# Who multiplies q and k by their reciprocal roots, and in which order: GpSimd and VectorE in a two-layer decoder trunk

## The chip, the cores and the metric

The kernel runs on one core of one Trainium2 chip. The metric is the device time of one execution in microseconds (us), median of three runs. A difference of 0.2% is about what a measurement of this kernel can tell from no change.

## The reference, cut to what matters

Two transformer layers over 512 tokens of width 1024. In both, the heads (64 wide) of q and k are normalised by their root mean square before attention:

```python
def rms_norm(x, gain):
    y = xf * lax.rsqrt(jnp.mean(xf * xf, axis=-1, keepdims=True) + EPS)
    return (y * gain)

# layer 0: 8 heads "A" (dilated windows), 8 heads "B" (window 128, 2 kv heads, sinks)
aq = rms_norm(aq.reshape(bsz, seq, N_HEADS_A, HEAD_DIM), a_q_gain)   # ak, bq, bk likewise
# layer 1: 16 heads "C" (forgetting attention)
q = rms_norm(proj[..., :w].reshape(bsz, seq, N_HEADS_C, HEAD_DIM), c_q_gain)   # k likewise
```

After each layer's attention there is an output projection and a squared-ReLU MLP (1024 to 4096 to 1024).

## The kernel before, in words

All large products are made in float32 from two parts, a rounded part (`whi`) and the rest (`wlo`), as three matmuls (L234 to L236, L165 to L169). The weights come by DMA into `wraw` (four buffers) and are split into `whi` and `wlo` (seven buffers each) by ScalarE, GpSimd or VectorE (L151, L153, L156). In the attention stages the pattern `PAT_ATT` gives every `whi` to GpSimd and the `wlo` by turns to VectorE and GpSimd.

`project` (L212) multiplies all four blocks of 128 tokens by a group of weight columns; the results stand in four PSUM banks `pj`. For a group of q and k its `use` calls `norm_heads` (L243):

- ScalarE copies the four banks to two tiles `qk` of shape [128 tokens, 2 blocks, 512 columns] and squares them (L250, L254); VectorE sums the squares by head (L255).
- `rsqrt_small` (L120) computes the reciprocal root on VectorE, eleven short instructions on up to 36 columns a token; its result is `rs` (in the first call `room`).
- `normalise` (L271) multiplies `qk` by `rs`, block by block, in place. `NORM = 'vgvg'` gives blocks 0 and 2 to VectorE and blocks 1 and 3 to GpSimd; each instruction takes all columns of its block (512, or 128 for the two k heads of B).

`norm_heads` is called eight times. In this text the calls are named **start** (A, first four heads: 256 columns of q and 256 of k; its multiplications are put off until the first v projection has ended, L283 and L524), **kB** (two k heads of B), **qB** (eight q heads of B), **A1** (A, last four heads) and **C0** to **C3** (layer 1, four heads each, q and k).

`prep_q` and `prep_k` (L293, L304) then transpose 128 columns, that is one pair of heads, of all four blocks on TensorE (`head_T`, L290: four transposes into one bank `qkT`), split the result on ScalarE and VectorE (L300, L301, L160, L161), and for k swap halves with a DMA (L313). The first pair needs columns 0 to 127 of q and, where q and k stand in one tile, columns 256 to 383 for k. Scores follow (L348 to L351), softmax (L362 to L373), transposes of the probabilities (L385), values (L405 to L409).

A generator `run` (L453) mixes steps of attention with matmuls of the next projection in program order. The order on each engine is then planned when the kernel is built, by program order and by the planner's own costs; only instructions under `in_order` or `keep_in_program_order` are pinned behind the one traced before them on their engine. [...]

Of the kernel before, what the change touches and what calls it, by code (L numbers as in the profile page):

```python
# [18 lines left out]
P = 128  # L19
# [3 lines left out]
NT = S // P  # L23
FF = 4096
HD = 64
# [9 lines left out]
R = 6  # L35
PAT_START = (('act', 'dve'), ('act', 'dve'))
WARM = 30
NORM = 'vgvg'
PSC = 'ggga'
GRAIN = 4  # L40
TABLES0 = 6
# [19 lines left out]
LEADS = (0.0, 0.0, -0.16, 0.33, -0.3, -0.23, -0.09)  # L61
# [8 lines left out]
def trunk(ctx, tc, x, b_sinks, w_out_even, b_forget, w_out_odd, w_up, w_down, xt, gains, w_in_even, w_in_odd, out):  # L70
    nc = tc.nc
# [72 lines left out]
    def in_order(m):  # L144
        if cnt["start"]:
            tc.keep_in_program_order(m)
# [50 lines left out]
    def layer_attention(li, hT, w_in, w_out, stats=None):  # L197


        with ExitStack() as c2:  # L200
# [39 lines left out]
                use(outs)  # L240
                yield 0

            def norm_heads(outs, nh, sq_tag="sq", sq_bufs=1 + li, ms=None):  # L243


                w = nh * HD
# [22 lines left out]
                                            op0=OP.mult, op1=OP.add)  # L269
                rsqrt_small(rs, v, room)  # L270
                def normalise():  # L271
                    for t in range(NT):
                        q = qk[t // 2][:, t % 2, :w].rearrange("p (h d) -> p h d", d=HD)
                        eng = nc.gpsimd if NORM[t] == "g" else nc.vector
                        m = eng.tensor_mul(q, q, rs[:, t, :nh].unsqueeze(2).to_broadcast([P, nh, HD]))
                        if eng is nc.vector:
                            in_order(m)

                if ms is None:
                    normalise()  # L280
# [168 lines left out]
            def chain(*gens):  # L449
                for g in gens:  # L450
                    yield from g

            def run(att, n_att, dense, n_dense, lead=0.0):  # L453

                a = d = 0
                while True:
                    if d / n_dense <= (a + lead * n_att) / n_att or att is None:
                        c = next(dense, None)
                        if c is None:
                            break  # L460
                        d += c
                    else:
                        if next(att, "end") == "end":
                            att = None
                        a += 1
                if att is not None:
                    for _ in att:
                        pass
# [56 lines left out]
                    cnt["start"] = False  # L525
                return use

            def qk_use(key, nh, *sq):
                def use(outs, ms=None):
                    st["qk", key] = norm_heads(outs, nh, *sq, ms=ms)  # L530
                return use

            def all_of(gen):
# [3 lines left out]
            if li == 0:  # L537
# [25 lines left out]

                start(ap, hT, w_in, make_tables(ap, dist, lt, lb), [bank("pA", f"pj{t}") for t in range(NT)], qk_use(0, 8, "P3", 2))
                all_of(v_a(0))
                run(att_a(0), 32, chain(kv_b(), project([(1536, 2048)], qk_use("b", 8))), 768, LEADS[0])
                run(att_b(), NB, chain(qk_a(1), v_a(1)), 768, LEADS[1])
                run(chain(att_a(1), last_values()), 38, chain(out_part([0, 1, 4, 5], True),
                                                              out_part([6, 7], False), ahead([2, 3])), 1536, LEADS[2])
# [714 lines left out]
```

## Time and profile before

| | us |
|---|---|
| median of the runs (three, 1161.77 to 1162.87) | 1161.94 |
| the profiled execution, its own time | 1160.99 |
| its span, first to last instruction | 1159.2 |

The span is nearly all TensorE: the two attention stages lie at about 28 to 215 us and 590 to 820 us, the MLPs behind them. The profiled execution is 0.95 us below the median.

### The profile page before, as it was taken

The numbers are of one execution on the slowest core, as the hardware profiler recorded it, in microseconds if no ns is written. First come the engines' busy times: TensorE is split into PE (matmuls) and PEld (weight loads), VectorE is DVE, ScalarE is ACT, GpSimd is POOL, SyncE is SP. The second block draws the span as 40 slices with busy tenths as digits, with TensorE's granted clock in tenths as the row PEclk, the third lists the DMA queues.
The fourth block names the chain that finished last, engine by engine and source line by source line (L and its number), as shares of the span: only waits on it lengthen the run. The fifth ranks groups of instructions, "written<-read, shape, count | busy, mean of one in ns | idle before, by whom it ended". The sixth has DMA issues, their size and how long they took to land.

```text
span 1159.2 us, 17365 instructions
## 1 busy us (share of the span) xinstructions
PE 1141.9 (99%) x6228; PEld 977.8 (84%) x6228; DVE 873.0 (75%) x1865; ACT 645.2 (56%) x1342; POOL 198.1 (17%) x292
## 2 busy tenths in 40 slices
PE   9999999999999999999999999999999999999998
PEld 7887887888989988988988888888888888888887
DVE  7878899969868857855647877778858759669676
ACT  7555867655545455444335685655756455465452
POOL 0445434100000000000255545332100000000000
PEclk9999999999999999999999999999999999999999
DMA  8432114232333332433443433343420722523403
GB/s 288 131 91 74 55 38 146 75 108 91 93 108 92 112 105 76 123 96 111 147 128 109 110 101 98 111 129 117 161 86 18 230 80 67 188 73 111 147 34 109
DMA packets 94695, 126.57 MB, mean 109 GB/s; under 512 B 5888, under 2 KB 66304, under 8 KB 94608
## 3 DMA queue, kind: packets, MB, share of 16 engines
q1 hardware_dynamic: 93568, 123.29, 34.7%
q10 hardware_dynamic: 1040, 2.16, 0.5%
q8 instruction: 49, 0.80, 0.3%
q14 instruction: 38, 0.31, 0.1%
HBM read 114.39 MB, written 4.23 MB: 102 GB/s over the span
## 4 chain that ended last, share of the span: by engine, by line
PE 84%; DVE 8%; DMA 3%; ACT 2%; issue 2%; POOL 1%; SPq 0%; POOLq 0%; DVEq 0%; ACTq 0%
PE up L165 10%; PE up L169 10%; PE up L168 10%; PE pj L236 4%; PE pj L234 4%; PE pj L235 4%; PE O L405 3%; PE PT L385 2%; PE op L169 2%; PE op L165 2%; PE op L168 2%; PE Y L1045 2%; PE Y L1042 2%; PE Y L1044 2%; PE Y L1091 1%
## 5 line engine op out<-in xcount | busy, mean ns | idle before, releaser
L165 PE MATMUL up<-xin,whi 128*128 128x512 f32 x512 | 200.6, 392 | 0.0
L169 PE MATMUL up<-xin,whi 128*128 128x512 f32 x512 | 199.4, 389 | 0.0
L168 PE MATMUL up<-xin,wlo 128*128 128x512 f32 x512 | 199.3, 389 | 0.0
L791 ACT CAST whi<-wraw 128x512 fp32r<-128x512 f32 x228 | 139.2, 619 | 105.1 <-PE up L169 47.7
L792 DVE TENSOR_TENSOR wlo<-wraw,whi 128x512 fp32r<-128x512 f32 x228 | 151.6, 685 | 50.9 <-ACT whi L791 50.7
L169 PEld LDWEIGHTS up<-xin,whi 128*128 128x128 f32 x512 | 96.1, 188 | 20.1
L168 PEld LDWEIGHTS up<-xin,wlo 128*128 128x128 f32 x512 | 96.2, 188 | 19.9 <-issue 0.2
L165 PEld LDWEIGHTS up<-xin,whi 128*128 128x128 f32 x512 | 96.2, 188 | 19.6 <-issue 0.2
L365 ACT ACTIVATE P<-P,negm 128x128 f32<-128x128 f32 (+5 forms) x128 | 69.5, 543 | 42.7 <-DVE negm L362 40.3
L973 ACT ACTIVATE u<-up 128x512 f32<-128x512 f32 x64 | 38.3, 598 | 90.9 <-PE up L169 90.9
L234 PE MATMUL pj<-whi,hn 128*128 128x512 f32 (+2 forms) x256 | 88.7, 347 | 0.0
L236 PE MATMUL pj<-whi,hn 128*128 128x512 f32 (+2 forms) x256 | 87.0, 340 | 0.0
L235 PE MATMUL pj<-wlo,hn 128*128 128x512 f32 (+2 forms) x256 | 86.9, 339 | 0.0
L153 POOL TENSOR_SCALAR whi<-wraw 128x512 fp32r<-128x512 f32 x88 | 59.7, 680 | 158.7 <-PE pj L236 137.6
L812 DVE TENSOR_TENSOR t<-u 128x256 f32<-128x256 f32 x56 | 23.2, 423 | 62.8 <-ACT u L1116 61.1
L156 POOL TENSOR_TENSOR wlo<-wraw,whi 128x512 fp32r<-128x512 f32 x48 | 63.8, 1332 | 21.4 <-ACT whi L151 18.9
L156 DVE TENSOR_TENSOR wlo<-wraw,whi 128x512 fp32r<-128x512 f32 (+1 forms) x71 | 49.0, 698 | 18.6 <-POOL whi L153 15.1
L373 POOL TENSOR_SCALAR P<-P,rden 128x256 f32<-128x256 f32 (+2 forms) x96 | 48.0, 503 | 82.8 <-DVE rden L368 77.2
L397 ACT CAST PT<-PT 128x256 fp32r<-128x256 f32 (+3 forms) x128 | 48.9, 403 | 20.3 <-PE PT L385 19.4
L362 DVE CUSTOM_DVE_ANT_0 P<-S,bias 128x128 f32<-128x128 f32 (+1 forms) x96 | 45.7, 484 | 17.4 <-PE S L351 11.8
L791 ACT CAST whi<-mraw 128x512 fp32r<-128x512 f32 x64 | 38.8, 620 | 33.1 <-DVE mraw L902 14.4
L385 PE MATMUL PT<-ident,P 128*128 128x128 f32 x296 | 53.4, 276 | 2.4 <-DVE negm L362 1.4
(241 smaller groups left out, 3083.5 us busy)
## 6 DMA issues: line engine op xcount, KB each, us to landing
wraw<-in_w_up SPq DMA_DIRECT2D x64, 512.0 KB, 4.3
wraw<-in_w_down SPq DMA_DIRECT2D x56, 512.0 KB, 3.8
wraw<-in_w_in_odd SPq DMA_DIRECT2D x22, 512.0 KB, 3.8
wraw<-in_w_in_even SPq DMA_DIRECT2D x17, 512.0 KB, 5.0
mraw<-in_w_down SPq DMA_DIRECT2D x16, 512.0 KB, 4.7
K<-K SPq DMA_DIRECT2D x26, 256.0 KB, 2.9
bias<-csp SPq DMA_DIRECT2D x16, 256.0 KB, 3.3
wraw<-in_w_out_odd SPq DMA_DIRECT2D x8, 512.0 KB, 3.7
```

The source lines that it names most:

```text
L153: nc.gpsimd.tensor_scalar(dst_h, src, 1.0, 1.0, op0=OP.mult, op1=OP.mult)
L156: in_order((nc.gpsimd if lo == "pool" else nc.vector).tensor_sub(dst_l, src, dst_h.bitcast(F32)))
L165: m = nc.tensor.matmul(o, wh, xh, start=start, stop=False, skip_group_check=more)
L168: nc.tensor.matmul(o, wl, xh, start=False, stop=False, skip_group_check=more)
L169: nc.tensor.matmul(o, wh, xl, start=False, stop=stop, skip_group_check=more)
L234: nc.tensor.matmul(o, xh, hi[:, :n], start=k == 0, stop=False)
L235: nc.tensor.matmul(o, xh, lo[:, :n], start=False, stop=False)
L236: nc.tensor.matmul(o, xl, hi[:, :n], start=False, stop=k == DC - 1)
L365: nc.scalar.activation(p[:, :ne], p[:, :ne], AF.Exp, scale=-1.0, bias=negm[:, i:i + 1], accum_out=den[:, i:i + 1])
L385: nc.tensor.transpose(pt[:, (i - c) * P:(i - c + 1) * P], pr[i][:, kb * P:(kb + 1) * P], ident)
L791: sca(nc.scalar.copy(dst_h, src))
L792: late.append(lambda: vec(nc.vector.tensor_sub(dst_l, src, dst_h.bitcast(F32))))
```

## The change

It takes the pattern by blocks away and deals the columns out instead. VectorE multiplies the columns of the first pair of heads in all four blocks (four instructions): of 512 columns the first 128 of each half for `halves=2` (256 columns in all), the first 128 for qB, which passes `halves=1`, and all 128 for kB. Then, for all but kB, VectorE copies the roots from `rs` into `v` (a tile of the same small size that is no longer needed), pinned behind its last multiplication, and GpSimd multiplies the other columns of the four blocks (256 each, or 384 for qB), reading the roots from that copy.

```diff
-NORM = 'vgvg'
-            def norm_heads(outs, nh, sq_tag="sq", sq_bufs=1 + li, ms=None):
+            def norm_heads(outs, nh, sq_tag="sq", sq_bufs=1 + li, ms=None, halves=1):
...
                 def normalise():
-                    for t in range(NT):
-                        q = qk[t // 2][:, t % 2, :w].rearrange("p (h d) -> p h d", d=HD)
-                        eng = nc.gpsimd if NORM[t] == "g" else nc.vector
-                        m = eng.tensor_mul(q, q, rs[:, t, :nh].unsqueeze(2).to_broadcast([P, nh, HD]))
-                        if eng is nc.vector:
-                            in_order(m)
+
+                    def mul(eng, hs, rs):
+                        for t in range(NT):
+                            q = qk[t // 2][:, t % 2, :w].rearrange("p (s h d) -> p s h d", s=halves, d=HD)[:, :, hs]
+                            r = rs[:, t, :nh].rearrange("p (s h) -> p s h", s=halves)[:, :, hs]
+                            m = eng.tensor_mul(q, q, r.unsqueeze(3).to_broadcast([P, halves, hs.stop - hs.start, HD]))
+                            if eng is nc.vector:
+                                in_order(m)
+
+                    mul(nc.vector, slice(0, 2), rs)
+                    if nh > 2 * halves:
+                        tc.keep_in_program_order(nc.vector.tensor_copy(v[:, :, :nh], rs[:, :, :nh]))
+                        mul(nc.gpsimd, slice(2, nh // halves), v)
...
-            def qk_use(key, nh, *sq):
+            def qk_use(key, nh, *sq, halves=2):
                 def use(outs, ms=None):
-                    st["qk", key] = norm_heads(outs, nh, *sq, ms=ms)
+                    st["qk", key] = norm_heads(outs, nh, *sq, ms=ms, halves=halves)
...
-                run(att_a(0), 32, chain(kv_b(), project([(1536, 2048)], qk_use("b", 8))), 768, LEADS[0])
+                run(att_a(0), 32, chain(kv_b(), project([(1536, 2048)], qk_use("b", 8, halves=1))), 768, LEADS[0])
```

## Rows read from the trace of the kernel before

**Rows 1.** The page, parts 1 and 2: TensorE's busy time with its share of the span and its count, and the clock granted to it in 40 slices (tenths of full speed).

```profile
PE 1141.9 (99%) x6228; PEld 977.8 (84%) x6228; DVE 873.0 (75%) x1865; ACT 645.2 (56%) x1342; POOL 198.1 (17%) x292
...
PEclk9999999999999999999999999999999999999999
```

**Rows 2.** The page, part 4: the chain of work that ended last, share of the span by engine.

```profile
PE 84%; DVE 8%; DMA 3%; ACT 2%; issue 2%; POOL 1%; SPq 0%; POOLq 0%; DVEq 0%; ACTq 0%
```

**Rows 3.** Who made TensorE wait over the whole span: us in total, times, longest.

```profile
PE S L348 <- DMA K<-K: 1.7, 2, 1.2
...
PE S L348 <- DVE yf L409: 1.2, 1, 1.2
PE qkT L290 <- DVE qk L275: 1.2, 2, 0.7
PE qkT L290 <- POOL qk L275: 1.1, 2, 0.5
```

**Rows 4.** The multiplications, all instructions of L275: duration in ns (least, median, most), first and last start, shapes. The two of `room` are those of start.

```profile
L275 DVE TENSOR_TENSOR qk<-qk,rs x14: 293/1138/1537, 67.5 to 752.9; 128x512 f32<-128x512 f32 x12, 128x128 f32<-128x128 f32 x2
L275 POOL TENSOR_TENSOR qk<-qk,rs x14: 435/1488/1549, 67.6 to 753.8; 128x512 f32<-128x512 f32 x12, 128x128 f32<-128x128 f32 x2
...
L275 POOL TENSOR_TENSOR qk<-qk,room x2: 1047/1048/1049, 39.2 to 40.2; 128x512 f32<-128x512 f32 x2
...
```

**Rows 5.** Timeline of qB, by engine (VectorE, GpSimd, TensorE): start, busy us, instruction, and in brackets the idle time before it with what ended it.

```profile
99.97 2.14 DVE L275 TENSOR_TENSOR qk<-qk,rs 128x512 f32<-128x512 f32 x2
...
100.02 2.99 POOL L275 TENSOR_TENSOR qk<-qk,rs 128x512 f32<-128x512 f32 x2 [0.52 <-DVE rs L135]
...
99.77 0.39 PE L236 MATMUL pj<-whi,h 128*128 128x512 f32 x1
100.81 0.30 PE L290 MATMUL qkT<-ident,qk 128*128 128x128 f32 x1 [0.65 <-DVE qk L275]
101.62 0.33 PE L290 MATMUL qkT<-ident,qk 128*128 128x128 f32 x1 [0.51 <-POOL qk L275]
...
102.25 0.27 PE L290 MATMUL qkT<-ident,qk 128*128 128x128 f32 x1
103.07 0.33 PE L290 MATMUL qkT<-ident,qk 128*128 128x128 f32 x1 [0.55 <-POOL qk L275]
```

**Rows 6.** Timeline of A1, VectorE and then TensorE, columns as in rows 5.

```profile
153.26 2.81 DVE L275 TENSOR_TENSOR qk<-qk,rs 128x512 f32<-128x512 f32 x2
156.10 0.68 DVE L409 TENSOR_TENSOR yf<-O,yf 64x512 f32<-64x512 f32 x1
...
155.21 0.40 PE L168 MATMUL op<-y,wlo 128*128 128x512 f32 x1
156.84 0.39 PE L348 MATMUL S<-K,Q 128*128 128x256 f32 x1 [1.23 <-DVE yf L409]
```

**Rows 7.** Timeline of start, GpSimd, VectorE and then TensorE, columns as in rows 5.

```profile
39.24 2.06 POOL L275 TENSOR_TENSOR qk<-qk,room 128x512 f32<-128x512 f32 x2 [1.57 <-issue]
41.27 1.20 POOL L153 TENSOR_SCALAR whi<-wraw 128x512 fp32r<-128x512 f32 x2
42.55 1.59 POOL L156 TENSOR_TENSOR wlo<-wraw,whi 128x512 fp32r<-128x512 f32 x1
...
41.92 1.09 DVE L156 TENSOR_TENSOR wlo<-wraw,whi 128x512 fp32r<-128x512 f32 x1 [0.73 <-POOL whi L153]
...
43.32 1.97 DVE L275 TENSOR_TENSOR qk<-qk,room 128x512 f32<-128x512 f32 x2
...
42.23 0.28 PE L234 MATMUL pj<-whi,h 128*128 128x256 f32 x1
43.45 0.39 PE L234 MATMUL pj<-whi,h 128*128 128x256 f32 x1 [0.95 <-DVE v L161]
...
44.03 0.28 PE L236 MATMUL pj<-whi,h 128*128 128x256 f32 x1
44.83 0.63 PE L290 MATMUL qkT<-ident,qk 128*128 128x128 f32 x4 [0.52 <-DVE qk L275]
```

**Rows 8.** Timeline behind the multiplications of C0 (GpSimd, VectorE, TensorE), and in the last line the same wait of VectorE behind C3.

```profile
611.91 0.62 POOL L153 TENSOR_SCALAR whi<-wraw 128x512 fp32r<-128x512 f32 x1
...
614.51 1.08 DVE L156 TENSOR_TENSOR wlo<-wraw,whi 128x512 fp32r<-128x512 f32 x1 [3.47 <-POOL whi L153]
...
619.08 0.39 PE L235 MATMUL pj<-wlo,hn 128*128 128x512 f32 x1
620.66 0.36 PE L348 MATMUL S<-K,Q 128*128 128x256 f32 x1 [1.20 <-DMA K<-K]
...
755.95 0.69 DVE L156 TENSOR_TENSOR wlo<-wraw,whi 128x512 fp32r<-128x512 f32 x1 [1.53 <-POOL whi L153]
```

**Rows 9.** Prices of like instructions. First the page's part 5 (busy us, mean ns of one): a product of 256 columns on VectorE; then two lines of instructions by source line or tile (ns least, median, most): the small copy behind the roots of start, and VectorE's `wlo` in the stage 28 to 215 us.

```profile
L812 DVE TENSOR_TENSOR t<-u 128x256 f32<-128x256 f32 x56 | 23.2, 423 | 62.8 <-ACT u L1116 61.1
...
L282 DVE COPY rcol<-room x1: 170/170/170, 39.1 to 39.1; 128x4 f32<-128x4 f32 x1
...
L156 DVE TENSOR_TENSOR wlo<-wraw,whi x24: 674/686/1524, 27.5 to 206.9; 128x512 fp32r<-128x512 f32 x24
```

**Rows 10.** Two loads into one tile `wraw`, whose column ranges (256 and 16 of each row of 272) interleave in it: issue of both on the DMA queue, and the time from issue to landing.

```profile
549.62 0.88 SPq L184 DMA_DIRECT2D wraw<-in_w_in_odd  x2
...
DMA to landing us min/median/max: 2.5/2.7/2.8
```

## The prediction

> **What bounds the kernel now.** I read the page first. [...] Second, the list of what TensorE waited for [rows 3]: the multiplications appear by name (1.2 us for VectorE's, 1.1 us for GpSimd's), and next to them waits that may hang on them (`yf`, the DMA of K). Third, the timelines around the eight calls, to see what each of these waits is. The ends of matmuls are modelled, so I take the lost time from start to start: matmuls of 512 columns follow each other at 0.23 us, of 256 at 0.12, transposes at 0.11.
>
> The reader is to see this in them. At **qB** four transposes stand in TensorE's queue ahead of projection work that could run, and block 0 waits for VectorE, blocks 1 and 3 for GpSimd. From 99.77 to 100.81, 100.81 to 101.62 and 102.25 to 103.07 that is 0.81 + 0.70 + 0.71 = 2.2 us lost [rows 5]. At **A1** the transposes come later; the loss is 155.21 to 156.84, 1.4 us, and it stands behind VectorE's `yf`, which waits in VectorE's queue behind 2.81 us of multiplications [rows 6]. At **start** TensorE loses 1.1 us (42.23 to 43.45) and 0.7 us (44.03 to 44.83) [rows 7]. At **C0** it loses 1.35 us to the DMA of K [rows 8]. kB, C1, C2 and C3 have no wait of TensorE for a multiplication.
>
> The multiplications themselves are slow because two engines do them at once: VectorE's 512 columns take up to 1.54 us [rows 4], where a VectorE product of that size, `wlo`, takes 0.67 to 0.69 (least and median) [rows 9]; GpSimd's take 1.05 us at start and up to 1.55 elsewhere [rows 4]. (At qB, 99.97 + 0.69 is 0.15 us before the first transpose, which I take as the hand-over [rows 5].)
>
> **The change, part by part.**
>
> *VectorE's share.* Removed: two instructions of 512 columns a call, together 2.14 us at qB and 2.81 at A1. Added: four of 256 columns at 0.42 us, taken from the product of that shape [rows 9], 1.7 us; at qB four of 128 columns at 0.29 us [rows 4], 1.2 us; and the copy, 0.17 us [rows 9]. GpSimd can start only behind the copy, so these four run without its multiplications beside them.
>
> *GpSimd's share.* Removed: two of 512 columns, 2.1 us alone [rows 7] and 3.0 us beside VectorE [rows 5]. Added: four of 256. The trace has no such shape; between 128 columns at 0.44 us and 512 at 1.05 [rows 4] a straight line gives 0.64 us, and 0.85 for 384. So 2.6 us (qB 3.4), ending about 1.7 + 0.2 + 2.6 = 4.5 us after the roots instead of 3.0. It is nobody's first need: the second pair is transposed many steps later.
>
> *qB.* The blocks are ready 0.29 us apart from 99.97 on. With the hand-over of 0.15 the first transpose starts at 100.41 and the second at 100.70; TensorE's two matmuls between the second and the third cover the rest. Left of the loss: 0.4 + 0.2. Gain 1.6 us; bounds 1.0 and 2.2 (all of it).
>
> *A1.* VectorE starts its four at 153.26 too, is through at 154.95, with the copy at 155.12, and `yf` starts there instead of at 156.10. Gain 1.0 us; bounds 0 (the plan puts the four elsewhere) and 1.4.
>
> *start.* GpSimd's multiplications stand ahead of two `whi`; behind these wait VectorE's `wlo` at 41.92, the last `v` and TensorE's 1.1 us [rows 7]. They will stand behind them now, which lets the `whi` start sooner, by 2.06 us at most; when TensorE frees their buffers the rows don't show, so I count on a part of it. On the other side VectorE has four blocks to do before block 3 can be transposed, where it had two, and the first of them still meets GpSimd's `wlo` of 42.55: 1.7 us alone against the 1.97 seen. I take a gain of 0.5 us; bounds -0.3 and 1.2.
>
> *C0.* GpSimd's `whi` at 611.91 waited only for the multiplications; VectorE stood 3.47 us for a later `whi` of that queue, with Q and K behind it, and TensorE's 1.35 us hang on that K [rows 8]. Afterwards GpSimd is free for 1.9 us between roots and copy and can make one `whi` there, but its multiplications end later. I take a gain of 0.3 us; bounds -1.4 and 1.35.
>
> *kB, C1 to C3.* kB: four of 0.29 us all on VectorE, 1.2 us; its k is first used by B's attention, which comes behind A's and the projection of qB in program order, and is covered by these; without them it costs 1.2 us at most. C1 to C3: nothing, covered by projection matmuls; without that cover each would gain about 1 us like A1.
>
> *What moves.* GpSimd's multiplications still need time beside VectorE; they now meet VectorE's next work. VectorE's `wlo` takes 0.69 us alone and 1.09 beside a GpSimd `wlo`, at most 1.52 [rows 7, 9]. I take one such loss of 0.4 us that reaches TensorE; bounds 0 and 3.4 (0.84 us at each of the four places where TensorE's loss hangs on VectorE).
>
> [...]
>
> Sum: 1.6 + 1.0 + 0.5 + 0.3 - 0.4 = 3.0 us. On the profiled execution's own 1160.99 that is 1158.0; it lies 0.95 us under the median of the runs, so for a median I predict 1161.94 - 3.0 = **1158.9 us**.
>
> **The rivals.**
>
> *The collision is only moved* (no change). At qB, A1, start and C0 a `wlo` or another product of VectorE's meets GpSimd's longer row of four, and 0.84 us is lost each time: 3.4 us against gains of 3.4, 1161.9 us; with half of it, 1160.2. For it: GpSimd's row lies where VectorE has work queued (busy 75% over the span). Against it: where TensorE hangs on VectorE at A1, VectorE's next instruction is `yf`, which reads PSUM and takes 0.68 us there, no more than `wlo` alone [rows 6, 9]. The planned order may shift as well and lose the same elsewhere.
>
> *GpSimd is late for its `whi`* (slower). It makes all `whi` of these stages. If the four multiplications stay ahead of the next `whi` in its queue, that `whi` comes 4.5 - 3.0 = 1.5 us later, VectorE's `wlo` with it, and what stands behind that in VectorE's queue. VectorE waits so at start, C0 and C3 [rows 7, 8]; qB's row would be the longest of all. Price 1.5 us a place, 6.0 at all four, less the gains of qB and A1, 2.6: 1165.3 us. It decides (0.2%, 2.3 us, slower) from the fourth place on; with three it is 1163.8. For it: the 3.47 us at C0. Against it: seven buffers of `whi` give much lead, and the copy comes so late that ready `whi` can pass first.
>
> *The first pair does not get free* (the change doesn't do what it says; slower). If the framework orders instructions by whole blocks of a tile, the transposes of the first pair wait for GpSimd's other columns too. Then qB's last transpose comes at 99.97 + 1.2 + 0.2 + 3.4 = 104.8 in place of 103.07 and start's at 43.32 + 1.7 + 0.2 + 2.6 = 47.8 in place of 45.3, 4.2 us, less A1's 1.0: 1165.1 us. Against it: the transpose of block 0 at qB ran while GpSimd still wrote block 1 of the same tile [rows 5], and two loads into interleaved columns of one tile left 0.05 us apart though the first took 2.5 us to land [rows 10].
>
> **How the numbers follow.** Forecast 0.58 (its own range 1156 to 1160.3: the bounds of qB, A1, start and C0 above), collision moved 0.22, GpSimd late 0.13, first pair not free 0.07. The forecast lies beyond 0.2% (below 1159.6) in most of its cases, 0.50, and within in 0.08. The first rival gives 0.04 faster, 0.16 same and 0.02 slower; the second 0.04 same and 0.09 slower; the third 0.07 slower. Together 0.54 faster, 0.28 same, 0.18 slower. The range reaches from the sum with the higher bounds, 1155.0, up to 1164.5, which holds the first rival and the second with three places; about 0.15 lies above and little below.
>
> **What would show it.** Right: VectorE's multiplications of 256 columns at about 0.42 us in one row with the copy behind, GpSimd's at 0.6 to 0.9 behind that; at qB a loss of TensorE of 0.6 us in place of 2.2 and no wait for GpSimd's `qk`; at A1 the wait for `yf` nearly gone. Wrong: transposes of a first pair that wait for GpSimd; VectorE's waits for `whi` longer than 0.7, 3.5 and 1.5 us; new waits of TensorE for scores or for K in layer 1, or multiplications of VectorE that still last twice their time alone, because some other GpSimd work lies beside them. A shift of the planned order in stages where nothing was to change would make the prediction wrong with its mechanism right.

## The result and the profile after

The changed kernel takes 1165.93 us (median of 10 runs, 1164.46 to 1168.98) against 1161.97 for the kernel before (10 runs beside it, 1160.96 to 1163.25): ratio 1.0037, 95% interval 1.0029 to 1.0046. It is 0.37% slower, 4.3 us by the ratio, where 3 us faster were predicted, and it lies above the predicted range. The profiled execution took 1164.64 us, 1.3 us under the median, with a span of 1162.9.

TensorE's busy time from the page of the changed kernel answers to [rows 1]; behind it stand two stretches of that trace (us, TensorE's busy time, granted clock as a share of full speed, share and GB/s of the DMA):

```profile
PE 1143.6 (98%) x6228; PEld 979.2 (84%) x6228; DVE 876.1 (75%) x1888; ACT 646.3 (56%) x1342; POOL 196.7 (17%) x304
...
188.30:190.40 2.10, 0.00 (x0) 1.00 0.89 259
190.40:193.80 3.40, 2.83 (x12) 0.50 0.99 308
```

The span is 3.7 us longer than before, and not all of that is time in which TensorE stands still: from 190.4 to 193.8 us, which takes in the end of the kernel's longest wait and the matmuls behind it, the granted clock stood at 0.50. The page's row of 40 slices doesn't show it (9 stands for 90% or more there). In the trace of before, read in windows of 1 us, none lies below 1.00.

The executions differ in this as well. The mean granted clock of the ten of the changed kernel lies between 0.995 and 1.000, and the times go with it: the five at 0.999 and 1.000 took 1164.46 to 1166.46 us, the five below 1165.28 to 1168.98. Of 125 executions of the kernel before, run beside the experiments, 114 had 0.999 or 1.000.

Whom TensorE waited for in the changed kernel (us in total, times, longest) answers to [rows 3]:

```profile
PE S L354 <- DMA K<-K: 5.6, 4, 2.7
PE qkT L296 <- DVE qk L276: 2.6, 2, 1.7
```

GpSimd's multiplications are gone as a cause, and so is `yf`. In their place the scores wait for the DMA of K: 5.6 us at four places, where it was 1.7 at two. One wait of 2.7 us is the longest of the kernel. The transposes wait 2.6 us for VectorE alone, about as much as for both engines together before (1.2 + 1.1).

The multiplications of the changed kernel (ns least, median, most; first and last start) answer to [rows 4]:

```profile
L276 DVE TENSOR_TENSOR qk<-qk,rs x28: 280/417/1380, 67.6 to 757.2; 128x256 f32<-128x256 f32 x20, 128x128 f32<-128x128 f32 x8
L276 POOL TENSOR_TENSOR qk<-qk,ssv x24: 612/618/1066, 103.1 to 759.9; 128x256 f32<-128x256 f32 x20, 128x384 f32<-128x384 f32 x4
L276 DVE TENSOR_TENSOR qk<-qk,room x4: 409/428/1492, 42.5 to 44.6; 128x256 f32<-128x256 f32 x4
```

The prices were right: 0.417 us for 256 columns on VectorE (0.42 predicted), 0.28 for 128 (0.29), 0.618 on GpSimd (0.64). But single ones still last 1.4 to 1.5 us: beside what?

**kB.** VectorE and then GpSimd in the changed kernel (start, busy us, instruction):

```profile
67.57 2.41 DVE L276 TENSOR_TENSOR qk<-qk,rs 128x128 f32<-128x128 f32 x4
70.02 0.68 DVE L307 TENSOR_TENSOR Q<-qkT,Q 64x512 fp32r<-64x512 f32 x1
...
67.68 0.66 POOL L152 TENSOR_SCALAR whi<-wraw 128x512 fp32r<-128x512 f32 x1 [4.79 <-PE pj L235]
68.43 1.41 POOL L155 TENSOR_TENSOR wlo<-wraw,whi 128x512 fp32r<-128x512 f32 x1
```

Four multiplications of 128 columns take 2.41 us, not the 1.2 of the prediction. GpSimd, which has no multiplication here any more, rounds and splits weights beside them. The last multiplication, the 1.38 us one, ends at 69.98, GpSimd's `wlo` at 69.84. Q and K of A's second pair, queued behind on VectorE, come 1.4 us later than before, and TensorE waits for that K (0.94 us from start to start).

**qB.** The same for qB, VectorE and then GpSimd; it answers to [rows 5]:

```profile
100.85 1.15 DVE L134 SCALAR_TENSOR_TENSOR rs<-rsq 128x32 f32<-128x32 f32 x1
102.04 0.90 DVE L276 TENSOR_TENSOR qk<-qk,rs 128x128 f32<-128x128 f32 x4
102.85 0.17 DVE L282 COPY ssv<-rs 128x32 f32<-128x32 f32 x1
...
100.69 1.26 POOL L155 TENSOR_TENSOR wlo<-wraw,whi 128x512 fp32r<-128x512 f32 x1
103.10 3.20 POOL L276 TENSOR_TENSOR qk<-qk,ssv 128x384 f32<-128x384 f32 x4 [1.15 <-DVE ssv L282]
```

VectorE's four take 0.90 us of busy time, less than the 1.2 predicted, and the copy 0.17. But the last operation of the roots, on 32 columns, takes 1.15 us in place of about 0.2 and ends at 102.00, as GpSimd's `wlo` ends at 101.95. Before, GpSimd stood at the head of its queue with its multiplications, waiting for these roots; its `wlo` was queued behind. Now its multiplications wait for the copy, the planner puts the `wlo` ahead of them, and it meets the roots.

**A's second group, second pair.** This place is none of the eight calls. VectorE, GpSimd and TensorE of the changed kernel:

```profile
182.57 1.09 DVE L155 TENSOR_TENSOR wlo<-wraw,whi 128x512 fp32r<-128x512 f32 x1 [1.39 <-POOL whi L152]
...
184.19 1.52 DVE L155 TENSOR_TENSOR wlo<-wraw,whi 128x512 fp32r<-128x512 f32 x1
185.74 0.68 DVE L307 TENSOR_TENSOR Q<-qkT,Q 64x512 fp32r<-64x512 f32 x1
...
181.92 1.21 POOL L152 TENSOR_SCALAR whi<-wraw 128x512 fp32r<-128x512 f32 x2 [3.90 <-DMA wraw<-in_w_out_even]
...
187.89 0.39 PE L164 MATMUL op<-y,whi 128*128 128x512 f32 x1
190.97 0.55 PE L354 MATMUL S<-K,Q 128*128 128x256 f32 x1 [2.69 <-DMA K<-K]
...
193.88 0.48 PE L354 MATMUL S<-K,Q 128*128 128x512 f32 x1
```

And VectorE of the kernel before at the same place:

```profile
182.53 0.68 DVE L301 TENSOR_TENSOR Q<-qkT,Q 64x512 fp32r<-64x512 f32 x1
...
187.43 2.12 DVE L156 TENSOR_TENSOR wlo<-wraw,whi 128x512 fp32r<-128x512 f32 x2
```

Before, Q and K stood ahead of the two `wlo` in VectorE's queue. Now two `wlo` stand ahead of Q; the first waits for GpSimd's `whi`, which waits for a weight load. Q starts at 185.74 in place of 182.53, and TensorE loses 2.85 us from start to start (190.97 - 187.89 less 0.23). Before, it lost 1.58 us at this pair, behind its scores, to `negm`. The granted clock falls to 0.50 while TensorE waits here (the stretch from 190.4 us above), so the first scores and transposes of the pair, from 190.97 to 193.88, run at 0.50. **What changed here is the order that the planner wrote.** The two programs' instruction lists, compared with buffer numbers left out, differ in 182 lines on TensorE, and on VectorE and GpSimd too, most of them between qB and the end of layer 0's attention.

**C0.** VectorE and GpSimd; it answers to [rows 8]:

```profile
611.99 1.17 DVE L133 TENSOR_TENSOR rsq<-rsq 128x32 f32<-128x32 f32 x1
...
618.05 1.09 DVE L155 TENSOR_TENSOR wlo<-wraw,whi 128x512 fp32r<-128x512 f32 x1 [3.11 <-POOL whi L152]
...
611.77 1.33 POOL L155 TENSOR_TENSOR wlo<-wraw,whi 128x512 fp32r<-128x512 f32 x1
```

As at qB, one operation of the roots is stretched to 1.17 us beside GpSimd's `wlo` (another to 0.65 beside its `whi`), and the wait of TensorE for K behind it is 1.95 us from start to start, against 1.35.

### The profile page after: what moved, and what is told of

It is laid out like the page before. It is cut to its first block, busy times and chain, and to the rows that moved or that the text cites. A ratio compares the mean times of both kernels' runs of the same rounds, so it can differ in the third digit from the quotient of the medians.

```text
span 1162.9 us, 17405 instructions
## 1 busy us (share of the span) xinstructions
PE 1143.6 (98%) x6228; PEld 979.2 (84%) x6228; DVE 876.1 (75%) x1888; ACT 646.3 (56%) x1342; POOL 196.7 (17%) x304
## 3 DMA queue, kind: packets, MB, share of 16 engines
q10 hardware_dynamic: 1040, 2.16, 0.5%
## 4 chain that ended last, share of the span: by engine, by line
PE 83%; DVE 7%; ACT 3%; DMA 3%; issue 2%; POOL 1%; SPq 0%; POOLq 0%; ACTq 0%; DVEq 0%
PE up L164 10%; PE up L168 10%; PE up L167 10%; PE pj L235 4%; PE pj L234 4%; PE pj L233 3%; PE O L411 2%; PE PT L391 2%; PE op L168 2%; PE op L164 2%; PE op L167 2%; PE Y L1051 2%; PE Y L1050 2%; PE Y L1048 2%; PE S L354 2%
```

## The experiments

What differs between the kernels is who multiplies what, and in which order. Times are ratios to the kernel before, run beside them (its medians 1161.28, 1161.68, 1161.55 and 1161.50 us in the four sessions, 27 to 33 runs each), and in brackets the 95% interval, turned into us:

| run | what is dealt the new way | ratio | us against before |
|---|---|---|---|
| only_kB | kB | 1.0009 | +1.0 (0.1 to 2.1) |
| only_qB | qB | 1.0027 | +3.1 (2.0 to 4.3) |
| only_A1 | A1 | 0.9998 | -0.2 (-1.2 to 0.8) |
| only_C | C0 to C3 | 1.0007 | +0.8 (-0.1 to 1.9) |
| only_start | start | 0.9996 | -0.5 (-1.5 to 0.5) |
| no_qB | all but qB | 1.0006 | +0.7 (-0.5 to 1.7) |
| kB_three | kB, GpSimd keeps one | 1.0002 | +0.2 (-0.8 to 1.3) |
| qB_two | qB, two pairs each | 0.9998 | -0.2 (-1.3 to 0.8) |
| qB_direct | qB, two pairs each, no copy | 0.9997 | -0.3 (-1.4 to 0.6) |
| qB_early | qB, late pair prepared earlier | 1.0009 | +1.0 (0.0 to 2.0) |
| old_early | none, late pair prepared earlier | 0.9999 | -0.1 (-1.2 to 0.8) |
| qB_pinned | qB, one place of the order put back | 1.0008 | +0.9 (-0.1 to 2.0) |
| all_pinned | all, one place of the order put back | 1.0007 | +0.8 (-0.2 to 1.9) |
| direct_all | all, no copy | 1.0079 | +9.2 (7.7 to 10.7) |
| start_qB | start, and qB as in qB_direct | 0.9993 | -0.8 (-1.9 to 0.2) |
| start_qB_A1 | start, A1, and qB as in qB_direct | 0.9990 | -1.2 (-2.2 to -0.1) |

The second reading is by place: the start of the same scores on TensorE in each trace, less that in the trace of before (us), at the scores that start there at the time in the head row. A trace as a whole can lie up to 0.7 us off from its beginning on, so differences along a row count, not its level. In the four rows with qB's new order (the changed kernel, only_qB, qB_pinned, all_pinned) 3, 6 and 8 matmuls fewer lie ahead of the scores at 105, 137 and 172 us, and as many as before at 196: up to 1.8 us of work is only put off there. These rows are compared with each other at those places, not with zero.

| trace | 55 | 74 | 105 | 137 | 172 | 196 | 623 | 794 |
|---|---|---|---|---|---|---|---|---|
| changed kernel | +0.1 | +1.1 | -0.1 | -0.8 | -0.6 | +3.1 | +3.7 | +3.6 |
| only_kB | +0.7 | +1.7 | +1.7 | +1.7 | +1.7 | +1.1 | +1.2 | +1.3 |
| only_qB | +0.5 | +0.5 | -0.8 | -1.5 | +0.7 | +4.9 | +4.8 | +5.2 |
| qB_pinned | +0.2 | +0.2 | -0.9 | -1.6 | -0.4 | +0.5 | +0.5 | +1.1 |
| all_pinned | +0.5 | +1.5 | +0.3 | -0.4 | -0.3 | +0.6 | +1.3 | +1.5 |
| start_qB_A1 | 0.0 | 0.0 | -0.4 | -0.1 | -0.7 | -1.5 | -1.4 | -1.5 |

**One call at a time.** A name for each call and a list of those that are dealt the new way:

```diff
+NEW = ('kB',)
...
+                    if call not in NEW:
+                        for t in range(NT):
+                            q = qk[t // 2][:, t % 2, :w].rearrange("p (h d) -> p h d", d=HD)
+                            eng = nc.gpsimd if t % 2 else nc.vector
...
```

> Only B's keys (kB) are dealt the new way: VectorE makes all four of their multiplications, GpSimd none; the seven other calls stay as before, and apart from these multiplications the order of every engine's instructions is that of the kernel before. Collision theory: GpSimd, no longer held at its two multiplications until the roots are there, runs its weight split beside VectorE's four multiplications, one of which stretches to about 1.4 us as in the changed kernel; A's second pair's Q and K come about 1.2 us later and a wait of TensorE of about 0.9 us at their first scores appears. Time +0.7 to +1.1 us, 1162.7 to 1163.1 against 1161.97. Rival (the prediction's own term): kB is covered by the attention and the qB projection and costs nothing, 1161.9 to 1162.1.

> Only B's queries (qB) are dealt the new way. This edit also makes the planner write another order for the rest of layer 0's attention: some 180 lines of TensorE's list and 125 of VectorE's stand differently, and it is this order, bar the other edits, that the changed kernel has. Order theory: the wait at B's first scores shrinks by 1 to 1.6 us, as predicted, and the new order gives back more than that at A's second pair of the second group, where two weight splits stand ahead of Q on VectorE: net +0.5 to +1.5 us, 1162.5 to 1163.5. Collision theory (the order is harmless, the losses of the changed kernel are single stretched instructions): the gain stays, 1160.3 to 1161.0.

> Only A's second group's first pair (A1) is dealt the new way; the order after it changes in 36 lines of TensorE's list and 19 of VectorE's, all behind it. The prediction's own term: the 1.4 us loss of TensorE at yf goes, -1.0 us (0 to -1.4), 1160.6 to 1162.0. Rival (what is saved at yf is waited for at the next thing, the scores' negm and the late second pair): 0 to +1 us, 1162.0 to 1163.0.

> Only layer 1's four calls (C0 to C3) are dealt the new way; layer 0 is the kernel before, and the order of layer 1 changes at the multiplications alone. Collision theory: C0's roots stretch beside GpSimd's weight split (two of them to 0.65 and 1.2 us) and the first scores wait 0.6 us longer, C3 loses 0.4 us more; +0.6 to +1.0 us, 1162.6 to 1163.0. The prediction's own term: C0 gains 0.3, C1 to C3 nothing, 1161.5 to 1161.8.

kB costs 1.0 us, all of it between 55 and 74 us, as the collision theory had it. qB alone costs 3.1 us, more than either theory expected. Against qB_pinned, which has the same order but for one place, its scores lose 0.9 us more between 137 and 172 us and 3.3 us more between 172 and 196. The second place is the one seen in the changed kernel; at the first the two kernels have the same order. At both the granted clock of only_qB was 0.50, from 158.2 to 161.6 us and from 192.3 to 195.7 (qB_pinned: 1.00), and this execution lies 1.5 us above the median of its kernel. VectorE and the wait of TensorE in only_qB:

```profile
185.59 1.50 DVE L157 TENSOR_TENSOR wlo<-wraw,whi 128x512 fp32r<-128x512 f32 x1
187.12 0.69 DVE L319 TENSOR_TENSOR Q<-qkT,Q 64x512 fp32r<-64x512 f32 x1
...
PE S L366 <- DMA K<-K: 5.2, 3, 3.1
```

A1 changes nothing that can be measured. Its wait at `yf` went and the next wait for `negm` grew by 0.3 us; between 137 and 196 us the trace keeps 0.4 us of the gain, less than the measurement can tell. TensorE's waits in only_A1, against 1.2 us for `yf` and 1.4 for `negm` before:

```profile
PE PT L403 <- DVE negm L380: 1.7, 1, 1.7
...
PE S L366 <- DVE yf L427: 0.2, 1, 0.2
```

Layer 1's +0.8 us can't be told from nothing. In that trace 0.4 us of it lie at C0. Another 1.1 us lie at 105 us, in layer 0, where nothing had changed: the granted clock was 0.50 there, from 103.5 to 106.9 us, behind the waits of qB, where it stayed at 1.00 in the trace of before. The stretched roots of C0, which I expected here, did appear; VectorE and GpSimd in only_C:

```profile
609.80 1.17 DVE L135 TENSOR_TENSOR rsq<-rsq 128x32 f32<-128x32 f32 x1
...
609.58 1.33 POOL L157 TENSOR_TENSOR wlo<-wraw,whi 128x512 fp32r<-128x512 f32 x1
```

TensorE lost 1.76 us to C0's K behind them. In the four traces whose C is dealt the new way with the copy it lost 1.76 to 2.16 us at this place, in the thirteen with the old dealing 1.30 to 1.59.

**Start alone, and all but qB.** The same list with other names.

> Only the first call (start) is dealt the new way; the order changes in 7 lines of TensorE's list. The prediction's own term: -0.5 us (-1.2 to +0.3). Rival (as the changed kernel's trace has it: the wait at the transposes gets shorter and the scores behind wait longer for the values' splits): -0.2 to +0.3 us.

> The changed kernel but for B's queries (qB), which are dealt the old way; the order behind them is near that of the kernel before (43 lines of TensorE's list differ, against 182). Order theory: 2.0 to 3.2 us of the changed kernel's +4.0 us come back; what stays is kB's 1.0 and layer 1's 0.4 to 0.8, +1.0 to +2.0 us against the kernel before. Rival (the collisions of all eight calls make up the loss, each about its share): at most 1 us comes back, +3 us or more.

Start measured -0.5 us, which is the prediction's own term but no more than its uncertainty; TensorE's loss of 1.11 us to `v` is down to 0.13, and that at the transposes is 1.07 in place of 0.68; the matmuls behind both come 0.54 us earlier. Without qB the change is within the uncertainty of no change, 3.6 us better than with it, a little more than the 2.0 to 3.2 expected. The parts add: 1.0 + 3.1 - 0.2 + 0.8 - 0.5 = 4.2 us, against 4.3 for the whole.

**kB: two more multiplications, or a freed GpSimd?**

```diff
-                            eng = nc.gpsimd if t % 2 else nc.vector
+                            eng = nc.gpsimd if (t == 3 if call == "kB" else t % 2) else nc.vector
```

> Only B's keys (kB) are dealt anew, but GpSimd keeps the last of the four multiplications; VectorE makes three. GpSimd then waits at the head of its queue for the roots as before, and its weight split (two inputs) can't start before its multiplication is done. Theory that the freed GpSimd is the cause: no multiplication of VectorE is stretched (three of 0.28 to 0.35 us), Q is at most 0.3 us later than before and the wait at A's second pair's first scores does not appear: -0.1 to +0.3 us. Rival (VectorE's two added multiplications are the cause): about three quarters of kB's loss stays, +0.6 to +0.9 us.

VectorE and then GpSimd in kB_three:

```profile
67.99 1.31 DVE L278 TENSOR_TENSOR qk<-qk,rs 128x128 f32<-128x128 f32 x3
69.34 0.69 DVE L319 TENSOR_TENSOR Q<-qkT,Q 64x512 fp32r<-64x512 f32 x1
...
68.11 0.43 POOL L278 TENSOR_TENSOR qk<-qk,rs 128x128 f32<-128x128 f32 x1 [4.80 <-DVE rs L136]
...
69.25 1.30 POOL L157 TENSOR_TENSOR wlo<-wraw,whi 128x512 fp32r<-128x512 f32 x1
```

One multiplication left to GpSimd is enough: GpSimd waits at it until the roots are there, its `wlo` starts at 69.25, when VectorE's three are done, and the wait of TensorE at the second pair is gone. The three take 1.31 us, not 0.9: two are still stretched, to 0.49 and 0.69 us, beside GpSimd's multiplication and its `whi`. The time (+0.2 us, -0.8 to 1.3) can't decide alone, but the trace does: the cause is the freed GpSimd, not VectorE's added work.

**qB: the dealing or the order?** A split of two pairs and two pairs leaves the order nearly as it was (12 lines of TensorE's list):

```diff
-                    mul(nc.vector, slice(0, 2), rs)
+                    mul(nc.vector, slice(0, 4), rs)
...
-                        mul(nc.gpsimd, slice(2, nh // halves), v)
+                        mul(nc.gpsimd, slice(4, nh // halves), v)
```

> Only B's queries (qB) are dealt anew, and VectorE takes the first two pairs of all blocks (four multiplications of 256 columns), GpSimd the last two. With this split the planner writes the order of the kernel before, but for 12 lines of TensorE's list and 3 of VectorE's. Order theory: the dealing is good and only the rewritten order of the run with the first pair alone was bad: four multiplications of 0.415 us end 1.66 us after the roots, about 1 us before the last transpose came before, so -0.6 to -1.2 us against the kernel before. Rival (what the dealing saves at B's first scores is waited for at the next thing, whatever the order): -0.2 to +0.3 us. Rival (the dealing itself harms, by contention): +0.5 us or more.

The 3 us are gone, but the gain doesn't come. VectorE and GpSimd in qB_two:

```profile
100.03 1.16 DVE L136 SCALAR_TENSOR_TENSOR rs<-rsq 128x32 f32<-128x32 f32 x1
101.22 1.43 DVE L287 TENSOR_TENSOR qk<-qk,rs 128x256 f32<-128x256 f32 x4
...
105.77 0.69 DVE L157 TENSOR_TENSOR wlo<-wraw,whi 128x512 fp32r<-128x512 f32 x1 [1.31 <-POOL whi L154]
106.49 0.69 DVE L319 TENSOR_TENSOR Q<-qkT,Q 64x512 fp32r<-64x512 f32 x1
...
99.88 1.26 POOL L157 TENSOR_TENSOR wlo<-wraw,whi 128x512 fp32r<-128x512 f32 x1
...
105.12 0.62 POOL L154 TENSOR_SCALAR whi<-wraw 128x512 fp32r<-128x512 f32 x1
```

The roots are stretched by 0.96 us as in the changed kernel. Then GpSimd's four multiplications hold up its next `whi`, VectorE's `wlo` waits for that and the second head's Q stands behind it: TensorE loses 1.35 us at those scores (0.39 before). That is the prediction's second rival, at a place it had not listed. From start to start TensorE loses 1.74 + 1.35 us here against 2.22 + 0.39 before.

In the next run GpSimd reads the roots themselves, so that it waits at its multiplications again, ahead of its `wlo`:

```diff
-                            tc.keep_in_program_order(nc.vector.tensor_copy(v[:, :, :nh], rs[:, :, :nh]))
-                        mul(nc.gpsimd, slice(4, nh // halves), v)
+                        mul(nc.gpsimd, slice(4, nh // halves), rs)
```

> Only B's queries (qB), VectorE the first two pairs of all blocks and GpSimd the last two, but GpSimd reads the roots themselves instead of the copy that waits for VectorE's multiplications. Its multiplications stand ahead of its weight split again, as in the kernel before, so the split can't run beside the last operation of the roots. Held-GpSimd theory: that operation takes 0.20 us instead of 1.16, the next weight rounding is no later than before (near 104.4), so Q of the second head isn't held behind it; VectorE's multiplications are stretched by GpSimd's, to between 0.45 and 0.9 us each; net -0.4 to -1.0 us against the kernel before. Rival (the two engines' multiplications stretch each other by as much as the split stretched the roots): -0.2 to +0.5 us.

The multiplications of qB_direct, between 100.2 and 103.6 us (ns least, median, most):

```profile
L287 DVE TENSOR_TENSOR qk<-qk,rs x4: 424/830/832, 100.4 to 102.2; 128x256 f32<-128x256 f32 x4
L287 POOL TENSOR_TENSOR qk<-qk,rs x4: 790/792/847, 100.4 to 102.7; 128x256 f32<-128x256 f32 x4
```

The last operation of the roots takes 0.19 us again, as expected, and now the two rows of multiplications stretch each other, to 0.83 us on VectorE. TensorE loses 0.77 + 0.38 + 0.44 + 0.44 at the transposes and 0.66 at the second head's scores, 2.7 in all, against 2.6 before. The rival holds: GpSimd's work for this stage is the same in both runs, and it met VectorE's either way, on the roots in qB_two (1.16 us for 0.19) and on the multiplications here (0.83 for 0.42).

**All eight without the copy.** The same edit in the changed kernel, with its first-pair split.

> All eight calls are dealt as in the changed kernel, but GpSimd reads the roots themselves, without the copy and its wait. The order behind B's queries is rewritten as in the changed kernel. Held-GpSimd theory: GpSimd waits at its multiplications again, so the roots of qB and C0 are no longer stretched, about 1 us back at each at most, while the two engines' multiplications stretch each other; the late second pair of A's second group stays: +2.0 to +3.5 us against the kernel before. Rival (the copy is what the change needs, without it the multiplications collide throughout): +4 us or more.

The held-GpSimd theory fell here; the rival holds: 9.2 us slower. The multiplications of qB, between 101.7 and 105.4 us, as above:

```profile
L287 DVE TENSOR_TENSOR qk<-qk,rs x4: 294/912/918, 101.8 to 103.7; 128x128 f32<-128x128 f32 x4
L287 POOL TENSOR_TENSOR qk<-qk,rs x4: 872/873/931, 101.8 to 104.4; 128x384 f32<-128x384 f32 x4
```

The first multiplication of 128 columns takes its 0.29 us, each of the others 0.91, about as long as GpSimd's beside it (0.87). VectorE's four take 2.80 us together; in the changed kernel they took 0.90, behind roots stretched by 0.96, and the copy 0.17. So the copy is worth its place at qB. That explains a part; the late second pair (a wait of 3.2 us from start to start) is there too. The granted clock is a further part. It was 0.50 in three stretches behind waits, 10 us together; up to half of that, 5 us, is lost (an estimate from these rows, at half the clock; the one stretch of the changed kernel cost about 1.3 us). The columns are those of the result:

```profile
104.20:107.60 3.40, 2.96 (x8) 0.50 0.01 1
162.30:165.60 3.30, 3.14 (x14) 0.50 0.00 0
196.40:199.70 3.30, 3.07 (x14) 0.50 0.96 322
```

Which part of the 9.2 us each of these is was not tested.

**The late second pair.** First its preparation was traced earlier in the program, with qB's new dealing and, as a control, with the old one:

```diff
                         for i, _ in enumerate(scores(q, kk[j], j, kind, h, pr)):
+                            if EARLY is not None and (kind, h0, p_, j, i) == ("a", 4, 0, 1, EARLY):
+                                nxt = get(1)
                             yield
```

> Like the run with qB alone (VectorE the first pair of all blocks), but the second pair of A's second group is prepared earlier in the program: its Q and K are traced right behind the last scores of the first pair, ahead of the weight splits that stood before it on VectorE. Theory that the late Q and K of that pair are the loss: the 3.2 us wait at their first scores goes, 2.5 to 3.3 us of the 3.5 us come back, 0.0 to +1.0 us against the kernel before. Rival (the rewritten order is looser in many places): less than 1.5 us comes back, +2 us or more.

> The old dealing in all eight calls, with the second pair of A's second group prepared earlier, as in the run before this one: the control for that edit. It rewrites 119 lines of TensorE's order behind it. The kernel before loses 1.6 us at that pair: theory of the late pair: -0.3 to -1.2 us. If the early preparation in itself shuffles the order for the worse: 0 to +1.5 us.

Of qB's 3.1 us, 2.1 came back, between the two expectations; with the old dealing the edit changes nothing. But this edit rewrites the order behind it as well, and its trace has a stretch with the granted clock at 0.50 from 159.4 us on, so it settles little. The next one changes one place: the two weight splits are issued behind that pair's Q and K (10 lines of TensorE's list differ; a few instructions of the other engines move too, all between 182 and 212 us).

```diff
-        in_order((nc.gpsimd if lo == "pool" else nc.vector).tensor_sub(dst_l, src, dst_h.bitcast(F32)))
+        with tc.issue_after(cnt["behind"]) if lo != "pool" and "behind" in cnt else ExitStack():
+            m = (nc.gpsimd if lo == "pool" else nc.vector).tensor_sub(dst_l, src, dst_h.bitcast(F32))
+        in_order(m)
...
                     scale_split(k[r, 0], k[r, 1], pt[r], g[r])
+                    if pin:
+                        cnt["behind"] = last
```

(`last` is the second of the two instructions of `scale_split`; `pin` is set for the second pair of A's second group.)

> The run with qB alone, the first pair on VectorE, and one place of the order put back: the weight splits that VectorE makes for the output projection's next load are issued behind the second pair's Q and K of A's second group, as in the kernel before. 10 lines of TensorE's list differ from the run with qB alone. Order theory: the 3.2 us wait at that pair's first scores goes and 2.3 to 4.0 us of the 3.1 us come back: -0.9 to +0.8 us against the kernel before. Rival (the late pair is a symptom of work that is late anyway and another wait takes its place): less than 1.5 us comes back, +1.6 us or more.

> The changed kernel (all eight calls) with the same place of the order put back. Order theory: 1.8 to 3.0 us of its +4.0 us come back and kB's 1.0 and layer 1's 0.4 to 0.8 us stay: +1.0 to +2.2 us. Rival: less than 1.2 us comes back, +2.8 us or more.

VectorE and TensorE in qB_pinned, and the pair's first and seventh score matmul in all_pinned:

```profile
184.65 0.69 DVE L323 TENSOR_TENSOR Q<-qkT,Q 64x512 fp32r<-64x512 f32 x1 [1.98 <-ACT Q L322]
...
188.26 1.28 DVE L158 TENSOR_TENSOR wlo<-wraw,whi 128x512 fp32r<-128x512 f32 x2
...
187.88 0.39 PE L174 MATMUL op<-y,whi 128*128 128x512 f32 x1
189.11 0.35 PE L372 MATMUL S<-K,Q 128*128 128x256 f32 x1 [0.84 <-DMA K<-K]
...
189.21 0.35 PE L372 MATMUL S<-K,Q 128*128 128x256 f32 x1 [0.93 <-DMA K<-K]
...
190.84 0.50 PE L372 MATMUL S<-K,Q 128*128 128x512 f32 x1
```

The wait falls from 3.23 to 1.0 us. qB with this place put back is at +0.9 us in place of +3.1 (2.2 us back, a little less than the 2.3 to 4.0 expected), and in the whole change the same edit gives back 3.5 of 4.3 us, more than the 1.8 to 3.0 expected: with it, the changed kernel can't be told from the kernel before. In the table of shifts, the changed kernel goes from -0.6 to +3.1 between 172 and 196 us, all_pinned, with the same work put off, from -0.3 to +0.6. So that one place of the order is the largest loss. The two traces say what it consists of: 1.8 us of wait (2.85 against 1.09 us in all_pinned), and 1.3 us because the thirteen matmuls from the pair's first score matmul to its seventh take 2.91 us in the changed kernel, at a granted clock of 0.50, and 1.63 in all_pinned, where it stays at 1.00.

**What can be had of the gain.** The parts that neither rewrite the order much nor free GpSimd at qB, put together: start as in the change, qB as in qB_direct, then A1 too.

> Two calls are dealt anew: start as in the change, and qB with two pairs on VectorE and two on GpSimd, which reads the roots themselves. 21 lines of TensorE's list differ from the kernel before. If the parts add, -0.5 and -0.4 (each within the uncertainty of its own run): -0.5 to -1.3 us, a ratio of 0.9989 to 0.9996. If these were noise: -0.3 to +0.3 us.

> As the run before this one, and A1 dealt as in the change too, which by itself moved 0.9 us from the wait at yf to a later one. If the parts add: -0.5 to -1.3 us, as without A1. If A1's saving meets another place now: down to -2.0 us. If the order, 73 lines of which now differ, costs: 0 or more.

```diff
+NEW = ('start', 'qB', 'A1')
...
+                    own, copy = (4, False) if call == "qB" else (2, True)
+                    mul(nc.vector, slice(0, own), rs)
```

start_qB_A1 is 1.2 us faster than the kernel before (0.1 to 2.2) and beats both kernels, narrowly. Its shifts fall to -0.7 us at 172 and -1.5 at 196, so A1's saving seems to be kept in part. With so many kernels beside each other, one interval that just leaves out 1 is weak evidence; the trace, 1.5 us ahead from 196 us on, points the same way.

## Why the prediction was wrong

**The step that failed: the sum held the order fixed.** Every term was worked out at the eight calls, and the stages between them were taken to run as before. The text named the opposite twice, "the planned order may shift as well" in the first rival and a shift "in stages where nothing was to change" in its last lines, and gave it neither place nor price nor chance. It was the largest term: 3.5 us by all_pinned, at a pair that lies some 85 us behind the edit. The edit at qB alone brings it (only_qB); kB's leaves TensorE's list as it is, and that of C changes the lists of VectorE and GpSimd alone.

**The clock, at nothing.** The prediction's terms are all time in which TensorE stands still; none is for the clock, which doesn't fall in the row of before [rows 1]. In the changed kernel a wait of 2.85 us came with 3.4 us at a granted clock of 0.50, about 1.3 us more. How much of the median's 4.3 us is clock stays open: the one execution at 1.000 took 1164.73 us, 2.8 us above the median of before beside it.

**kB, costed at nothing.** It was 1.0 us (only_kB). The cover that was named, A's attention, is itself fed by VectorE's queue: A's second pair's Q and K stand behind the four multiplications. The bound of 1.2 us "without cover" was about right in size. The question that the prediction asked, when B's keys are first needed, was the wrong one; the right one was what is queued behind them.

**qB, a gain of 1.6 us.** The multiplications and the copy took what was predicted. But the roots, taken as fixed in time, ended 0.96 us later, because GpSimd was no longer standing at its multiplications: TensorE's wait there fell from 2.22 to 1.83 us only. The local loss of 0.6 us that was to be seen is seen nowhere. That the scores of qB come earlier in the new order (-0.8 us at 105 us in only_qB) is no gain: three matmuls, 0.7 us, were put behind them.

**What moves, 0.4 us.** The mechanism was right and its place wrong. The prediction looked for the collision behind the copy, where GpSimd's multiplications now lie. It came ahead of them, on the roots and on VectorE's own multiplications, from the `wlo` that used to be queued behind GpSimd's wait. One loss of 0.4 us was also too little: 0.9 us reached TensorE at kB and 0.4 to 0.8 at C0, and at qB the roots took 0.96 us more. In the changed kernel the stretched instructions end with GpSimd's `wlo`: the operation of qB's roots 0.05 us after it (102.00, 101.95), the multiplication of kB 0.14 us after (69.98, 69.84). Without GpSimd's work beside them such instructions took 0.2 us (the same operation before the change) and 0.28 us (the multiplications of qB).

**A1, 1.0 us.** `yf` went as early as predicted, and TensorE's 1.40 us at that place went with it, though 0.95 us for `negm` stand right behind it in the changed kernel (156.90 to 157.97). Measured alone, the kernel gained nothing that can be told (-0.2 us, -1.2 to 0.8): in only_A1 the wait for a later `negm` grew by 0.3 us, and where the rest went stays open. The bound of 0 holds, for another reason than the one given.

**start, 0.5 us:** -0.5 measured alone, not told apart from nothing, and 0.54 at its place in the trace. **C0, a gain of 0.3:** its wait for K grew by 0.6 in the changed kernel. **C1 to C3** moved by 0.4 us at most and not lastingly, as predicted.

**The rivals.** "The first pair not free" didn't happen: the transposes of qB waited for VectorE alone. "GpSimd late for its `whi`" didn't happen in the changed kernel (VectorE's wait at C0 fell from 3.47 to 3.11 us) but did in qB_two. "The collision is only moved" is what happened at qB and, in qB_direct, whichever way it was turned; with it alone the kernel would have come out about where all_pinned is, within the uncertainty of no change.

**The range.** Its lower end, 1155.0 us, is not the sum with the higher bounds (2.2 + 1.4 + 1.2 + 1.35 = 6.15 us, 1155.8), and the lower bounds with the 0.4 us of "what moves" (1.0 + 0 - 0.3 - 1.4 - 0.4) give 1163.0, not the 1160.3 of the forecast's own range. The measured median lies above either.

## What to carry to other kernels

In a kernel whose order a planner writes, compare the order of the two programs before summing up durations: a local edit may be paid for at a place far behind it, where one instruction has passed another. A wait at the head of an engine's queue also held back what was behind it here: at qB GpSimd's `wlo` started at 103.49 us in qB_direct, behind the multiplications that waited for the roots, and at 99.88 in qB_two, ahead of them. When such a wait is taken away, ask what that work will collide with, and look ahead of the moved instructions as well as behind them. Where an edit is costed at nothing because its result is needed late, look at what is queued behind it on its engine. Behind a long wait of TensorE, read the granted clock of that stretch alone, not of the page's slices: here about 1.3 us came on top of a wait of 2.85.

## What the runs showed of the hardware

Three short instructions of VectorE's lasted in the changed kernel about as long as what was left of the one GpSimd `wlo` beside them: the last operation of qB's roots 1.15 us, with 1.10 us of the `wlo` left at its start; one operation of C0's roots 1.17, with 1.11 left; kB's last multiplication 1.38, with 1.24 left. Others of the same shapes took 0.19 and 0.28 us. Where both engines ran rows of multiplications, each lasted about as long as the one beside it: VectorE's of 128 columns 0.91 us beside GpSimd's of 384 at 0.87 (direct_all), those of 256 columns 0.83 beside GpSimd's of 256 at 0.79 (qB_direct), where the first of each row took 0.29 and 0.42. A smaller share for VectorE saved nothing there: its four took 2.80 us in direct_all and 2.68 in qB_direct.

TensorE's granted clock fell to 0.50 in the midst of waits (at 190.4 us in the changed kernel, in a wait that ended at 190.97) or behind them, in some executions and not in others: with the same order of TensorE's matmuls it was 0.50 from 103.5 to 106.9 us in only_C and 1.00 there in the trace of before. The same thirteen matmuls took 2.91 us at 0.50 in the changed kernel and 1.63 at 1.00 in all_pinned.
